# Up-projection by one level of Strassen's scheme in an encoder layer's MLP; its result goes through DRAM and the down-projection is a phase of its own

## Chip, cores and metric

The kernel runs on one core of a Trainium2 chip. The time is device microseconds of one execution, as the median of the runs shown: 2044.52 us (three runs, 2044.26 to 2045.95).

## What is computed

One layer of a hybrid encoder for 1024 prompt tokens and 8 x 16 sample tokens, 1152 rows in all, width 1024, inner MLP width 4096, in fp32. Attention, a gated delta network and their merge come first; the change touches only the channel mixer at the end, which runs on both groups of tokens:

```python
def channel_mixer(x, pre_g, post_g, w_up, w_down):
    h = rmsnorm(x, pre_g)
    u = jnp.square(jax.nn.relu(h @ w_up))
    return x + rmsnorm(u @ w_down, post_g)
```

## The kernel before

Every large product is made of three matmuls on TensorE. An fp32 operand is split into a high part in the type fp32r (`hi`, an ACT cast, L326) and the remainder (`lo`, a DVE subtraction, L327); `mm3` (L147-150) adds hi x hi, hi x lo and lo x hi in one PSUM accumulator. All matmuls named L150 are such.

Tokens are nine tiles of 128 (NTT), the width is eight pieces of 128 (KT), the inner width 32 rows of 128, each called an ft. The normalised input h stands transposed in SBUF as `hhi` and `hlo` [128, 9, 8, 128], in a pool on the right side of SBUF. The trace names these two `mhi` and `mlo` in this part of the program.

The out-projection stage (L1171-1216) goes tile by tile: 48 matmuls of 512 columns, a norm, the residual x1 stored to DRAM (L1209), a second norm (L158-175, its last operation L174), and eight 128x128 transposes (L183) whose results an ACT cast (`mhi`, L186) and a DVE subtraction (`mlo`, L187) write. A tile's transposes are emitted four tiles later than its matmuls (LAG).

The MLP (L1219-1288) is eight blocks of four ft. For each ft the up half loads two 256 KB pieces of w_up (L335, SP's queue), splits them, and runs 72 matmuls of 384 columns, 24 for each third of the tokens (`gemm_t`). Each third is evacuated by an ACT Relu (L1235) and a POOL square (L1236), and split into `uhi` and `ulo`, which stay in SBUF for the block. Two pieces of w_down (L1246) are split into `dhi` and `dlo`. The down half runs 18 accumulators (nine token tiles by two halves of the width), 12 matmuls of 512 columns each (L1260-1263); ACT copies the result to `yacc` in the first block (L1268) and DVE adds it in the others (L1270). Beside the last block the post-norm and the output go tile by tile.

Within an engine the order is set by a scheduler from the order of the code and from priorities (`high_priority`); buffers of a pool come free tile by tile (`reuse_waits="tile"`). All loads and stores of this part are issued by SP in one order, and an issue that waits holds back what stands behind it. Matmul accumulators rotate over PSUM banks, four with the tag `mm` in the up half; a bank is written again when its evacuation has read it.

## Time and profile before

| | |
|---|---|
| median of three runs | 2044.52 us |
| profiled execution | 2042.67 us |
| its span in the profile | 2041.0 us |
| PE busy | 1959.9 us, 96% |
| weight loads (PEld) busy, beside the matmuls | 1769.8 us |
| DVE / ACT / POOL busy | 1010.0 / 839.7 / 317.5 us |
| first down-projection matmul of the MLP | 1283.63 us |
| end of the last matmul | 2031.69 us |

The profile gives starts in microseconds from the start of the span. A matmul's listed duration is longer than the distance to the next start, since matmuls overlap in the array; what a stream of them costs is read from the starts. In a row of the grouped views the columns are: line, engine, operation, output<-inputs, shape, count, then busy time and mean ns, then the engine's idle time just before them with what ended it. In the views by window the columns are length, the busy time of PE, weight load, DVE, ACT and POOL with counts, the granted clock of TensorE, the share of the DMA engines' time, and GB/s.

### The profile page before, as it was taken

The page shows a single profiled execution, that of the slowest core. Times are in us where ns is not written, and L with a number is a line of the kernel's source. Part 1 is how long each engine was busy: PE and PEld are TensorE (multiplying, and loading weights), DVE is VectorE, ACT ScalarE, POOL GpSimd, SP SyncE. Part 2 cuts the span into 40 slices and gives each one's busy share as a digit, 9 for nine tenths or more (in the row PEclk, how much of TensorE's full clock was granted, in tenths as well). Part 3 has the DMA queues.
Part 4 walks back from the last instruction along what each step waited for, and adds up shares of the span by engine and source line. Part 5 has one row for each costly group of instructions (what it writes and reads, how often), then busy time and mean ns, then how long its engine had stood idle before and what let it go on. Part 6 is the DMA issues. An engine that isn't in the chain of part 4 may idle for free.

```text
span 2041.0 us, 29371 instructions
## 1 busy us (share of the span) xinstructions
PE 1959.9 (96%) x10892; PEld 1769.8 (87%) x10892; DVE 1010.0 (49%) x2403; ACT 839.7 (41%) x1982; POOL 317.5 (16%) x453
## 2 busy tenths in 40 slices
PE   7989999999999899999899999999999999999998
PEld 6979898898898878778789789898989898989896
DVE  6457577775765476666454465032323232323227
ACT  5433464654636475655443445240303030303032
POOL 1141332513312200000022001010101010202010
PEclk9999999999999999999999999999999999999999
DMA  6142324224253643433553522020202020202024
GB/s 191 44 102 62 101 62 118 67 76 129 53 141 104 188 148 103 130 100 83 168 156 96 173 106 93 1 83 1 83 1 83 1 83 11 73 11 73 21 83 155
DMA packets 216300, 181.47 MB, mean 89 GB/s; under 512 B 51132, under 2 KB 193272, under 8 KB 216156
## 3 DMA queue, kind: packets, MB, share of 16 engines
q1 hardware_dynamic: 201888, 160.33, 27.6%
q10 hardware_dynamic: 14268, 19.25, 2.6%
q8 instruction: 86, 1.41, 0.3%
q14 instruction: 58, 0.48, 0.1%
HBM read 136.67 MB, written 42.87 MB: 88 GB/s over the span
## 4 chain that ended last, share of the span: by engine, by line
PE 79%; DMA 7%; DVE 5%; ACT 4%; issue 3%; POOL 1%; SPq 1%; DVEq 0%; ACTq 0%; POOLq 0%
PE mm L150 48%; PE mf L150 13%; PE pc L1011 2%; PE pa L150 1%; DMA wor<-in_w_out_dram 1%; PE pd L150 1%; PE pb L150 1%; PE pc L150 1%; DVE xs L610 1%; PE pe L150 1%; DMA be<-rows_o 1%; PE mm L1040 1%; PE pc L625 1%; PE mm L1061 1%; PE pb L1002 1%
## 5 line engine op out<-in xcount | busy, mean ns | idle before, releaser
L150 PE MATMUL mf<-hhi,wlo 128*128 128x384 f32 x744 | 262.6, 353 | 3.4 <-DVE wlo L327 3.4
L150 PE MATMUL mf<-hhi,whi 128*128 128x384 f32 x744 | 261.6, 352 | 1.8 <-ACT gst L211 1.8
L150 PE MATMUL mf<-hlo,whi 128*128 128x384 f32 x744 | 262.5, 353 | 0.0
L150 PE MATMUL mm<-mlo,whi 128*128 128x384 f32 x768 | 260.1, 339 | 0.3 <-DVE mlo L187 0.3
L150 PE MATMUL mm<-mhi,whi 128*128 128x384 f32 x768 | 260.3, 339 | 0.0
L150 PE MATMUL mm<-mhi,wlo 128*128 128x384 f32 x768 | 260.1, 339 | 0.0
L150 PE MATMUL mm<-dhi,ulo 128*128 128x512 f32 x576 | 224.1, 389 | 0.0
L150 PE MATMUL mm<-dlo,uhi 128*128 128x512 f32 x576 | 224.1, 389 | 0.0
L150 PE MATMUL mm<-dhi,uhi 128*128 128x512 f32 x576 | 224.1, 389 | 0.0
L1236 POOL TENSOR_TENSOR ur<-ur 128x384 f32<-128x384 f32 x96 | 84.1, 877 | 776.2 <-ACT ur L1235 657.2
L1270 DVE TENSOR_TENSOR yacc<-mm,yacc 128x512 f32<-128x512 f32 x126 | 87.1, 691 | 203.7 <-PE mm L150 203.0
L327 DVE TENSOR_TENSOR wlo<-raw,whi 128x512 fp32r<-128x512 f32 x166 | 115.6, 697 | 110.3 <-ACT whi L326 106.6
L326 ACT CAST dhi<-raw 128x512 fp32r<-128x512 f32 x64 | 38.9, 620 | 293.3 <-PE mm L150 269.9
L327 DVE TENSOR_TENSOR ulo<-ur,uhi 128x384 fp32r<-128x384 f32 x96 | 53.7, 560 | 211.0 <-ACT uhi L326 211.0
L326 ACT CAST whi<-raw 128x512 fp32r<-128x512 f32 x166 | 102.8, 620 | 118.8 <-PE mm L150 47.0
L150 PEld LDWEIGHTS mf<-hhi,wlo 128*128 128x128 f32 x744 | 141.9, 191 | 4.6 <-DVE wlo L327 4.3
L150 PEld LDWEIGHTS mm<-mlo,whi 128*128 128x128 f32 x768 | 144.2, 188 | 0.8 <-DVE mlo L187 0.5
L150 PEld LDWEIGHTS mm<-mhi,whi 128*128 128x128 f32 x768 | 144.2, 188 | 0.6 <-ACT whi L326 0.3
L150 PEld LDWEIGHTS mm<-mhi,wlo 128*128 128x128 f32 x768 | 144.2, 188 | 0.3 <-DVE wlo L327 0.3
L150 PEld LDWEIGHTS mf<-hhi,whi 128*128 128x128 f32 x744 | 141.9, 191 | 2.4 <-ACT gst L211 2.1
L150 PEld LDWEIGHTS mf<-hlo,whi 128*128 128x128 f32 x744 | 142.1, 191 | 0.7
L150 PEld LDWEIGHTS mm<-dhi,ulo 128*128 128x128 f32 x576 | 108.1, 188 | 22.5
(470 smaller groups left out, 4049.9 us busy)
## 6 DMA issues: line engine op xcount, KB each, us to landing
raw<-in_w_in_dram SPq DMA_DIRECT2D x86, 256.0 KB
raw<-in_w_up_dram SPq DMA_DIRECT2D x64, 256.0 KB
raw<-in_w_down_dram SPq DMA_DIRECT2D x64, 256.0 KB
gate_d<-gst ACTq DMA_DIRECT2D x48, 192.0 KB
ga<-gate_d SPq DMA_DIRECT2D x48, 192.0 KB
xt<-in_x_prompt_dram SPq DMA_DIRECT2D x16, 512.0 KB
fr_d<-gst ACTq DMA_DIRECT2D x36, 192.0 KB
y<-rows_n SPq DMA_DIRECT2D x16, 288.0 KB
```

Of the source, the lines that this page charges most:

```text
L150: T.matmul(out, a, b, start=first and i == 0, stop=last and i == n - 1)
L326: A.copy(h, raw)
L327: V.tensor_tensor(l, raw, f(h), ALU.subtract)
L610: (A.copy if h else V.tensor_copy)(xs[0:64, h], st_[64 * h:64 * h + 64])
L625: T.matmul(po[:, i * P:(i + 1) * P], xs[k0:].rearrange("p h c -> p (h c)"), qa[k0:, u].rearrange("p h c -> p (h c)"), start=True, stop=True)
L1002: T.transpose(tp[:, jj * 256 + qi * P:jj * 256 + qi * P + P], pr[qi][:, j * P:(j + 1) * P], ident)
L1011: T.matmul(acc[:, q0:256], v2[:, 2 * jp + jj, P * hh:P * hh + P], q[:, jj * 256 + q0:jj * 256 + 256], start=jp == 0 and jj == 0 and k == 0 ...
L1040: T.matmul(a[32 * b:32 * b + 32, P:384], qbd[:, b].rearrange("p h t -> p (h t)"), kt, start=True, stop=True)
L1061: T.matmul(o[:, bs], vc[:, 2 * b + i], pT[:, 1 + i, bs], start=False, stop=b == 3 and i == 1)
L1236: G.tensor_tensor(r, r, r, ALU.mult)
L1270: V.tensor_tensor(yacc[:, t, ns], acc, yacc[:, t, ns], ALU.add)
```

## The change

The up-projection takes the ft two by two (after four ft that are done in the old way). The product of a pair is seen as a 2x2 block product: the inner dimension 1024 in two halves of 512, the outputs in two ft of 128, and the tokens in two halves, namely the first and the second 64 columns of each token tile. Winograd's form of Strassen's scheme makes the four output blocks from seven block products instead of eight. It needs four sums of weight blocks (POOL, `w_ops`, for each pair) and four sums of blocks of h (`h_sums`, once, split into THI and TLO, which the program calls `th`). The 576 columns of a block are done in two groups, five tiles (320 columns) and four tiles (256 columns), 12 matmuls each: 168 matmuls a pair where there were 144 of 384 columns. The products that use blocks of h itself read five or four pieces of 64 columns; those that use `th` read consecutive columns. The running sums are made when a product is evacuated: ACT copies for the first, 14 DVE additions, then ACT Relu and ACT Square into `u`, a row of 1152 columns, which is stored to DRAM (`u_d`). All eight PSUM banks serve as accumulators in this part.

The down-projection starts when all pairs are done. Its pool `fin` takes the place of `hhi`, `hlo` and `th`. It loads each row of `u` from DRAM again, splits it, loads and splits w_down, and runs the same matmuls as before: eight blocks, 18 accumulators of 12 matmuls, and the same post-norm.

```diff
     wps.close()
-    wps_["w"] = ctx.enter_context(tc.tile_pool(name="wp2", bufs=1, reuse_waits="tile"))
+    wps2 = ctx.enter_context(ExitStack())
+    wps_["w"] = wps2.enter_context(tc.tile_pool(name="wp2", bufs=1, reuse_waits="tile"))
...
+    u_d = dr.tile([DFF // P, P, NT], F32, name="u_d")
+    TH = NTT * 64
+    GR = ((0, 5), (5, 9))
+    def halves_t(x):
+        return x.rearrange("p (t n) -> p t n", n=64)
+    ts_ = ctx.enter_context(ExitStack())
+    th = ts_.enter_context(tc.tile_pool(name="th", bufs=1, side="right", reuse_waits="tile"))
+    THI, TLO = ([th.tile([P, 4, TH], F32R, name=nm("th")) for _ in range(4)] for _ in range(2))
+    wps2.close()
+    with tc.tile_pool(name="up", bufs=1, reuse_waits="tile") as up:
+        wps_["w"] = up
+        WBUFS["w"] = (6, 5)
+        def h_sums(t0, t1):
+            n = t1 - t0
+            def B(h, i, j):
+                return f(h[:, t0:t1, 4 * i:4 * i + 4, 64 * j:64 * j + 64])
+            def tmp():
+                z = up.tile([P, 4, P], F32, tag="ws", bufs=3, name=nm("ws"))
+                return z.rearrange("p k (t n) -> p (k t n)", t=2).rearrange("p (t k n) -> p t k n", t=2, k=4)[:, :n]
+            def diff(a, b):
+                x, y = tmp(), tmp()
+                G.tensor_tensor(x, B(hhi, *a), B(hhi, *b), ALU.subtract)
+                G.tensor_tensor(y, B(hlo, *a), B(hlo, *b), ALU.subtract)
+                V.tensor_tensor(x, x, y, ALU.add)
+                return x
+            def rest(a, x):
+                y = tmp()
+                V.tensor_tensor(y, B(hhi, *a), x, ALU.subtract)
+                V.tensor_tensor(y, y, B(hlo, *a), ALU.add)
+                return y
+            def out(i, x):
+                hi, lo = (z[i][:, :, 64 * t0:64 * t1].rearrange("p k (t n) -> p t k n", n=64) for z in (THI, TLO))
+                split(x, hi, lo)
+            t1_ = diff((0, 1), (0, 0))
+            out(0, t1_)
+            t2_ = rest((1, 1), t1_)
+            out(1, t2_)
+            out(2, diff((1, 1), (0, 1)))
+            out(3, rest((1, 0), t2_))
+        N0 = 4
+        for ft in range(N0):
+            u = up.tile([P, NT], F32, tag="u", bufs=3, name=nm("u"))
+            def evu(c, acc, u=u):
+                cs = slice(c * CH, (c + 1) * CH)
+                A.activation(u[:, cs], acc, AF.Relu)
+                A.activation(u[:, cs], u[:, cs], AF.Square)
+            gemm_t(weights(halves(w_up[0], ft * P)), hhi, hlo, KT, evu, tag=("mm", 4))
+            S.dma_start(u_d[ft], u)
+            if ft == 0:
+                for t in range(0, NTT, 2):
+                    h_sums(t, min(t + 2, NTT))
+        banks()
+        def w_ops(pr):
+            with tc.high_priority(200):
+                a = {}
+                for i in range(2):
+                    for j, src in enumerate(halves(w_up[0], (2 * pr + i) * P)):
+                        a[i, j] = up.tile([P, 4, P], F32, tag="wr", bufs=6, name=nm("wr"))
+                        S.dma_start(a[i, j], src.rearrange("(k p) n -> p k n", p=P))
+            def add(x, y, op):
+                z = up.tile([P, 4, P], F32, tag="ws", bufs=3, name=nm("ws"))
+                G.tensor_tensor(z, x, y, op)
+                return z
+            def parts(x):
+                h, l = (up.tile([P, 4, P], F32R, tag="w" + z, bufs=5, name=nm("w" + z)) for z in "hl")
+                split(x, h, l)
+                return h, l
+            with tc.high_priority(100):
+                yield parts(a[0, 0])
+                s1 = add(a[1, 0], a[1, 1], ALU.add)
+                s2 = add(s1, a[0, 0], ALU.subtract)
+                yield parts(s2)
+                yield parts(add(a[0, 0], a[1, 0], ALU.subtract))
+                yield parts(a[1, 1])
+                yield parts(s1)
+                yield parts(add(a[0, 1], s2, ALU.subtract))
+                yield parts(a[0, 1])
+        def hop(i, j):
+            return (lambda k, t0, t1: [z[:, t0:t1, 4 * i + k, 64 * j:64 * j + 64] for z in (hhi, hlo)])
+        def top(i):
+            return (lambda k, t0, t1: [z[i][:, k, 64 * t0:64 * t1] for z in (THI, TLO)])
+        prods = (hop(0, 0), top(1), top(2), top(3), top(0), hop(1, 1), hop(1, 0))
+        for pr in range(N0 // 2, DFF // P // 2):
+            uu = [up.tile([P, NT], F32, tag="u", bufs=3, name=nm("u")) for _ in range(2)]
+            sm = [[], []]
+            for i, ((wh, wl), b) in enumerate(zip(w_ops(pr), prods)):
+                for c, (t0, t1) in enumerate(GR):
+                    n = 64 * (t1 - t0)
+                    o = pt("mm", 8)[:, :n]
+                    mm3(o, [p3 for k in range(4) for hi, lo in (b(k, t0, t1),) for p3 in (
+                        (wh[:, k], hi), (wh[:, k], lo), (wl[:, k], hi))])
+                    def plus(x, tag, r=None):
+                        if r is None:
+                            r = up.tile([P, 320], F32, tag=tag, bufs=2 + (tag == "sr"), name=nm(tag))[:, :n]
+                        if x is None:
+                            A.copy(r, o)
+                        else:
+                            V.tensor_tensor(r, o, x, ALU.add)
+                        return r
+                    def done(row, half, r):
+                        A.activation(r, r, AF.Relu)
+                        u = uu[row].rearrange("p (t n) -> p t n", n=P)[:, t0:t1, 64 * half:64 * half + 64]
+                        A.activation(u, halves_t(r), AF.Square)
+                    z = sm[c]
+                    if i == 0:
+                        z.append(plus(None, "s1"))
+                    elif i == 1:
+                        z.append(plus(z[0], "s2"))
+                    elif i == 2:
+                        z.append(plus(z[1], "s3"))
+                    elif i == 3:
+                        done(1, 0, plus(z[2], "sr"))
+                    elif i == 4:
+                        plus(z[1], None, z[1])
+                        done(1, 1, plus(z[2], None, z[2]))
+                    elif i == 5:
+                        done(0, 1, plus(z[1], None, z[1]))
+                    else:
+                        done(0, 0, plus(z[0], "sr"))
+            for i in range(2):
+                S.dma_start(u_d[2 * pr + i], uu[i])
+    ts_.close()
+    phs.close()
+    banks()
     FB = 4
-    with tc.tile_pool(name="up", bufs=1, reuse_waits="tile") as up:
-        yacc = None
+    fin = ctx.enter_context(tc.tile_pool(name="fin", bufs=1, side="right", reuse_waits="tile"))
+    yacc = fin.tile([P, NTT, D], F32, name="yacc")
+    gpost = fin.tile([P, D], F32, name="gpost2")
+    lss = fin.tile([P, 4], F32, name="lss")
+    lsq = fin.tile([P, 512], BF16, name="lsq")
+    dn = fin
+    if True:
         nb = DFF // (FB * P)
-        fin = None
         for blk in range(nb):
             us, wd = [], []
             for i in range(FB):
                 ft = blk * FB + i
-                urs = [up.tile([P, CH], F32, tag="ur", bufs=3, name=nm("ur")) for _ in range(3)]
-                uhi = up.tile([P, NT], F32R, tag="uhi", bufs=FB, name=nm("uhi"))
-                ulo = up.tile([P, NT], F32R, tag="ulo", bufs=FB, name=nm("ulo"))
-                def evu(c, acc, uhi=uhi, ulo=ulo, urs=urs):
-                    cs = slice(c * CH, (c + 1) * CH)
-                    r = urs[c]
-                    A.activation(r, acc, AF.Relu)
-                    G.tensor_tensor(r, r, r, ALU.mult)
-                    split(r, uhi[:, cs], ulo[:, cs])
-                gemm_t(weights(halves(w_up[0], ft * P)), hhi, hlo, KT, evu, tag=("mm", 4))
-                us.append((uhi, ulo))
                 with tc.high_priority():
-                    dhi = up.tile([P, D], F32R, tag="dhi", bufs=FB, name=nm("dhi"))
-                    dlo = up.tile([P, D], F32R, tag="dlo", bufs=FB, name=nm("dlo"))
+                    uhi = dn.tile([P, NT], F32R, tag="uhi", bufs=2 * FB, name=nm("uhi"))
+                    ulo = dn.tile([P, NT], F32R, tag="ulo", bufs=2 * FB, name=nm("ulo"))
+                    ur = dn.tile([P, NT], F32, tag="ur", bufs=2, name=nm("ur"))
+                    S.dma_start(ur, u_d[ft])
+                    split(ur, uhi, ulo)
+                    us.append((uhi, ulo))
+                    dhi = dn.tile([P, D], F32R, tag="dhi", bufs=2 * FB - 1, name=nm("dhi"))
+                    dlo = dn.tile([P, D], F32R, tag="dlo", bufs=2 * FB - 1, name=nm("dlo"))
                     for n in range(2):
                         ns = slice(n * 512, (n + 1) * 512)
-                        raw = wps_["w"].tile([P, 512], F32, tag="wr", bufs=2, name=nm("raw"))
+                        raw = dn.tile([P, 512], F32, tag="wr", bufs=2, name=nm("raw"))
                         S.dma_start(raw, w_down[0][ft * P:(ft + 1) * P, ns])
                         split(raw, dhi[:, ns], dlo[:, ns])
                 wd.append((dhi, dlo))
-            if blk == nb - 1:
-                phs.close()
-                fin = ctx.enter_context(tc.tile_pool(name="fin", bufs=1, side="right", reuse_waits="tile"))
-                gpost = fin.tile([P, D], F32, name="gpost2")
+            last = blk == nb - 1
+            if last:
                 S.dma_start(gpost, g_mlp_post[0].partition_broadcast(P))
-                lss = fin.tile([P, 4], F32, name="lss")
-                lsq = fin.tile([P, 512], BF16, name="lsq")
-            if yacc is None:
-                yacc = up.tile([P, NTT, D], F32, name="yacc")
             for t in range(NTT):
                 ts_ = slice(t * P, (t + 1) * P)
                 for n in range(2):
@@ -1262,7 +1407,7 @@
                     acc = mmt()
                     mm3(acc, [pr for (uh, ul), (dh, dl) in zip(us, wd) for pr in (
                         (uh[:, ts_], dh[:, ns]), (uh[:, ts_], dl[:, ns]), (ul[:, ts_], dh[:, ns]))])
-                    end = fin and t == NTT - 1
+                    end = last and t == NTT - 1
                     with tc.high_priority(200 if end else 0):
                         if blk == 0:
                             A.copy(yacc[:, t, ns], acc)
@@ -1270,7 +1415,7 @@
                             V.tensor_tensor(yacc[:, t, ns], acc, yacc[:, t, ns], ALU.add)
                     if end:
                         A.activation(lsq, yacc[:, t, ns], AF.Square, accum_out=lss[:, n:n + 1])
-                if not fin:
+                if not last:
                     continue
```

The change moves instructions at three places. The first is the beginning of the MLP. These are TensorE's rows there in the old order; `tp` are the transposes of the last token tiles, `mm_13279` an accumulator of the first ft:

```order
L150 MATMUL mm_13279<-mlo,whi_13246 128x384
L150 MATMUL mm_13279<-mhi,wlo_13247 128x384
L183 MATMUL tp_13214<-ident,mix_13083 128x128 x4
L150 MATMUL mm_13279<-mhi,whi_13246 128x384
L183 MATMUL tp_13221<-ident,mix_13083 128x128 x4
L150 MATMUL mm_13279<-mlo,whi_13246 128x384
L150 MATMUL mm_13279<-mhi,wlo_13247 128x384
L150 MATMUL mm_13308<-mhi,whi_13240 128x384
```

And in the new order:

```order
L183 MATMUL tp_13200<-ident,mix_12994 128x128 x4
L183 MATMUL tp_13207<-ident,mix_12994 128x128 x4
L183 MATMUL tp_13214<-ident,mix_13083 128x128 x4
L183 MATMUL tp_13221<-ident,mix_13083 128x128 x4
L150 MATMUL mm_13259<-mhi,whi_13249 128x384
L150 MATMUL mm_13259<-mlo,whi_13249 128x384
L150 MATMUL mm_13286<-mhi,whi_13249 128x384
```

The up matmuls no longer stand between the transposes but behind the last of them. On ACT the cast of the first w_up piece (`whi_13249`) stands behind the last `mhi` cast and the first `th` cast of the sums:

```order
L186 CAST mhi<-tp_13207 128x512
L186 CAST mhi<-tp_13214 128x512
L186 CAST mhi<-tp_13221 128x512
L326 CAST th_13234<-ws_13341 128x2x4x64
L326 CAST whi_13249<-raw_13247 128x512
L326 CAST whi_13255<-raw_13253 128x512
```

On SP the load of that piece, which stood among the loads of the out-projection's weights, now stands behind the last store of x1.

The second place is the end of a pair on TensorE, shown with waits. `mm_14819` is the last group of 256 columns of one pair; its first matmul stands in its place, and its other eleven stand behind product 4 of the next pair (`mm_15015` is that product's second group). The last rows of this are:

```order
L150 MATMUL mm_14819<-mhi,wh_14798 128x256
L150 MATMUL mm_14819<-mlo,wh_14798 128x256
L150 MATMUL mm_14819<-mhi,wl_14799 128x256
L150 MATMUL mm_15038<-mhi,wh_15034 128x320 [waits DVE_49,Activation_49]
L150 MATMUL mm_15038<-mlo,wh_15034 128x320
L150 MATMUL mm_15038<-mhi,wl_15035 128x320
```

The group behind it, `mm_15038`, uses the bank of `mm_14819`. Its wait for DVE is the wait for the addition that reads `mm_14819`. Such a place is there for each pair but the last.

The third place is the border between the phases, on SP, with waits. `u_17287` and `u_17286` are the last pair's rows, `ur` the reloaded rows, `raw` pieces of w_down:

```order
L1367 DMA u_d<-u_17287 128x1152 [waits DMAHW4_49,Activation_49]
L1367 DMA u_d<-u_17286 128x1152 [waits DMAHW5_49,Activation_49]
L1389 DMA ur_17574<-u_d 128x1152 [waits DMAHW6_49,PE_49]
L1389 DMA ur_17590<-u_d 128x1152 [waits DMAHW7_49,PE_49]
L1397 DMA raw_17580<-in_w_down_dram 128x512 [waits DMAHW0_49,PE_49]
L1397 DMA raw_17584<-in_w_down_dram 128x512 [waits DMAHW1_49]
L1402 DMA gpost_17569<-in_norm_mlp_post_dram 128x1024 [waits DVE_49,DMAHW2_49,PE_49,Pool_49]
L1389 DMA ur_17606<-u_d 128x1152 [waits DMAHW6_49,DMAHW3_49,DVE_49]
L1389 DMA ur_17622<-u_d 128x1152 [waits DMAHW7_49,DMAHW4_49,DVE_49]
L1397 DMA raw_17596<-in_w_down_dram 128x512 [waits DMAHW5_49,DMAHW0_49,DVE_49]
```

All loads of the down phase stand behind the stores of the last pair, where the loads for a block stood beside its up half before. The third `ur` waits for DVE, which frees its buffer.

## Prediction

> **What bounds the kernel now.** I read the page first, then the chain of waits, then the MLP stage in windows, then single matmul starts.
>
> ```profile
> span 2041.0 us, 29371 instructions
> PE 1959.9 (96%) x10892; PEld 1769.8 (87%) x10892; DVE 1010.0 (49%) x2403; ACT 839.7 (41%) x1982; POOL 317.5 (16%) x453
> 1240.86 0.70 DVE mlo L187
> 1241.57 0.04 issue
> 1241.61 4.26 PE mm L150 x23
> 1245.87 0.01 issue
> 1245.88 785.81 PE mm L150 x3960
> 1300.00:1400.00 100.00, 100.00 (x506) 91.59 (x505) 21.13 (x33) 28.95 (x53) 10.49 (x12) 1.00 0.15 43
> ```
>
> The chain's last link is TensorE alone: 3960 matmuls from 1245.88 to 2031.69 without a gap. A window inside it (columns: length, then busy time of PE, weight load, DVE, ACT, POOL, then clock, DMA share, GB/s) has PE at 100 of 100, full clock, the other engines under a third, DMA at 43 GB/s. So the MLP is worth what its matmuls cost, and a removed matmul pays at once, as long as nothing else becomes late. Here are the starts of the first matmul of down block 0, up block 1 and down block 1:
>
> ```profile
> 1283.63 0.39 PE L150 MATMUL mm<-dhi,uhi 128*128 128x512 f32 x1
> 1332.64 0.34 PE L150 MATMUL mm<-mhi,whi 128*128 128x384 f32 x1
> 1383.52 0.39 PE L150 MATMUL mm<-dhi,uhi 128*128 128x512 f32 x1
> 908.39 0.28 PE L1011 MATMUL pc<-plo,v 128*128 128x256 f32 x1
> 908.51 0.28 PE L1011 MATMUL pc<-phi,v 128*128 128x256 f32 x1
> 908.63 0.28 PE L1011 MATMUL pc<-plo,v 128*128 128x256 f32 x1
> ```
>
> A down block is 49.01 us for 216 matmuls of 512 columns, 226.9 ns each. An up block is 50.88 us for 288 matmuls of 384, 176.7 ns each. The attention's 256-column matmuls start 120 ns apart.
>
> **1. The matmuls that go.** The line through 256 and 512 columns has (226.9-120)/256 = 0.418 ns a column. It gives 146.7 ns at 320, and 173.4 at 384. The up matmuls take 176.7, and read their tokens from hi/lo tiles in three pieces of 128; I put the 3.3 ns on the two extra pieces, 1.65 ns each. In the new scheme four of seven products read whole rows (the sums in `th`): 12 x (146.7+120) ns = 3.20 us each. Three read `mhi`/`mlo` in five and four pieces of 64: 12 x (146.7+4x1.65+120+3x1.65) = 3.34 us each. A pair of ft is then 22.8 us, against 144 x 176.7 = 25.44 us: 2.62 us saved, times 14 pairs = **-36.7 us**. The ends: no price for pieces, 7 x 3.20, -42.6; the price on all seven, -28.8.
>
> The Trainium skill ("TensorE: Matmul & The Clock Gate", Part 2, "Back-to-back issue gap") has the isolated spacing as N/2.4 GHz plus about 2.5 ns, thus 109 ns at 256 columns. By it, with 136 ns at 320, a pair would be 20.6 us and this term -68 in place of -36.7. The trace disagrees with it, 120 ns measured, and I stay with the rows.
>
> **2. The start of the MLP.** Now the first up matmuls stand between the last transposes:
>
> ```profile
> 1134.43 0.43 SPq L335 DMA_DIRECT2D raw<-in_w_up_dram  x1
> ...
> 1222.42 13.29 SPq L1209 DMA_DIRECT2D x_d<-xt  x2
> 1242.18 0.99 SPq L335 DMA_DIRECT2D raw<-in_w_up_dram  x2
> 1245.20 0.62 ACT L326 CAST whi<-raw 128x512 fp32r<-128x512 f32 x1 [0.22 <-DMA raw<-in_w_up_dram]
> 1238.16 1.28 DVE L174 SCALAR_TENSOR_TENSOR mix<-xt,nss,gpre 128x1024 f32<-128x1024 f32 x1
> 1240.24 0.59 ACT L186 CAST mhi<-tp 128x512 fp32r<-128x512 f32 x1 [2.28 <-PE tp L183]
> 1242.67 0.69 DVE L187 TENSOR_TENSOR mlo<-tp,mhi 128x512 fp32r<-128x512 f32 x1
> L326 ACT CAST dhi<-raw 128x512 fp32r<-128x512 f32 x56 | 34.0, 620 | 289.8 <-PE mm L150 269.9 <-DMA raw<-in_w_down_dram 19.5
> L327 DVE TENSOR_TENSOR dlo<-raw,dhi 128x512 fp32r<-128x512 f32 x56 | 38.2, 692 | 67.7 <-ACT dhi L326 67.4
> L326 ACT CAST uhi<-ur 128x384 fp32r<-128x384 f32 x85 | 43.6, 513 | 83.6 <-POOL ur L1236 83.6
> L327 DVE TENSOR_TENSOR ulo<-ur,uhi 128x384 fp32r<-128x384 f32 x85 | 47.5, 559 | 194.9 <-ACT uhi L326 194.9
> L1235 ACT ACTIVATE ur<-mm 128x384 f32<-128x384 f32 x85 | 41.7, 490 | 83.3 <-PE mm L150 83.3
> L1236 POOL TENSOR_TENSOR ur<-ur 128x384 f32<-128x384 f32 x85 | 74.3, 874 | 628.8 <-ACT ur L1235 628.8
> ```
>
> The first up weights are loaded at 1134, long ahead. In the change the up pool opens after the out-projection stage: its first load stands on SP behind the last x1 store, whose issue ends at 1235.7, and its cast on ACT behind the last `mhi` cast and a first `th` cast, which waits for a DVE add behind the last `mlo`. All transposes go first. The norm of the last tile ends at 1239.44 as now; without the two `dhi` casts that stand between its two `mhi` casts, the last `mlo` ends near 1242.2 rather than 1243.4. Then the add (0.7), the `th` cast (0.62) and the `whi` cast (0.62) with their semaphores: the first up matmul at **1244.2**. The load, some 3 us from issue to use (1242.18 to 1245.20), is there by 1239 and hidden. Four plain ft take 50.88 us as now and end at 1295.1 where today's end at 1283.63: +11.4. Four loads of 256 KB leave the stage around 1134, worth nothing to 1 us there, I take -0.7. PE is nearly idle for up to 10 us; what that does to its clock is seen at 1016:
>
> ```profile
> 1016.00:1020.00 4.00, 2.24 (x6) 1.94 (x7) 1.97 (x4) 1.81 (x4) 0.00 (x0) 0.50 0.75 229
> 1020.00:1024.00 4.00, 3.54 (x10) 2.73 (x10) 2.30 (x4) 1.83 (x5) 0.00 (x0) 0.50 0.67 212
> 1024.00:1028.00 4.00, 3.71 (x13) 2.31 (x12) 2.30 (x4) 2.10 (x4) 0.00 (x0) 0.75 0.67 215
> 1019.15 0.53 PE L150 MATMUL pd<-ohi,whi 128*128 128x384 f32 x1
> 1019.47 0.53 PE L150 MATMUL pd<-olo,whi 128*128 128x384 f32 x1
> ```
>
> The granted clock is 0.50 and the 384-column matmuls start 0.32 us apart, not 0.17; full clock returns only after some us of dense work. I take one such stretch, 3.4 us of work at half clock that would take 1.7, so +1.7 (nothing to 3.4). The start is **+12.4 us**, 9 to 16. `h_sums` itself lies on DVE, ACT and POOL beside the plain ft (about 7.5 us for each of its five groups, done before 1295); without that cover each group would cost its 7.5.
>
> **3. The end of each pair.** Program order on PE leaves eleven matmuls of a pair's last group until after product 4 of the next pair; the next group reuses that bank and waits until DVE has read it. From the last start: the drain beyond the pace 0.28-0.12 = 0.16, the 256-column add (559 less 128 x 1.04 ns a column from the two lo rows) 0.43, two semaphores: 0.7 us, for 13 pairs **+9.1 us**. Queued behind it are the rest of this pair's matmuls, so nothing covers it. Ends: 0, if PE's queue hides it, and 18, if the add also finds a 0.69 us lo split ahead of it on DVE. Beside this the pair's own work fits: DVE 7 x 0.69 + 7 x 0.49 + 7 x 0.43 = 11.3 us, ACT 7 x 0.62 + 18 x some 0.4 = 11.5, POOL four 128x512 (874 ns at 384, so about 1.1) = 4.4, each within 22.8. Loads and stores are 2.2 MB a pair, about 97 GB/s. The 96 POOL squares that go were beside full PE: nothing.
>
> **4. Between the phases.** All down-phase tiles lie where `mhi`, `mlo` and `th` lay, and SP has the last pair's two stores ahead of the first `u` load. So no load starts before the last product is evacuated: add 0.43, Relu 0.38, Square 0.38, semaphores: the last store issues 1.45 us after the product's end.
>
> ```profile
> 741.28 5.35 DMA qv<-fr_d
> 811.31 7.31 DMA qv<-fr_d
> qv<-fr_d SPq DMA_DIRECT2D x8, 576.0 KB
> 10.00:20.00 10.00, 5.45 (x23) 4.10 (x23) 8.21 (x26) 7.22 (x16) 6.46 (x22) 1.00 0.96 298
> ```
>
> `qv` is a 576 KB load, the size of a `u` row. The first takes 5.4 us behind one issue: landed at +6.9; the second row and two w_down pieces share the queue at up to 298 GB/s: the last at +10.1. Casts of 1152 columns are 620 + 640 x 0.84 = 1.16 us on ACT, 1.36 on DVE. First down matmul +10.4, first ft done +14.2. Only two `ur` and two raw buffers exist and four banks, so PE can do four of 18 accumulators ft by ft (2.7 us of work), at about 6.3 us for an ft (lo split, issue, 2.8 us load, cast; the bytes alone, 1.6 MB with the loads between, are 5.6). Fourth ft done +33.1; then 14 accumulators x 12 x 226.9 ns = 38.1: block 0 ends at +71.2, not +49.0: +22.2. Idle and sparse work halve the clock here also, some 3.5: **+25.8 us**. Ends: 17.7 without the clock and with loads at the window's rate; 34 with each load like the 7.31 row and two clock stretches.
>
> **5. Later borders.** Two `u` rows and the fourth w_down of the next block stand behind a block's last accumulator: some 0.3 us x 7 = **+2**, 0 to 6. The tail from 2031.69 to 2041.0 keeps its instructions: 0.
>
> **Sum.** -36.7+12.4+9.1+25.8+2 = +12.6. The span would be 2053.6. The profiled execution is 1.67 us longer than its span, 2042.67, and 1.85 below the runs' median of 2044.52; on the median it is 2057.1. **Forecast 2057 us.**
>
> **The rivals.**
>
> A. The new waits are hidden, and the kernel is faster. Place: the pairs' ends and the phase border. Price: 0 for 9.1 and 17.7 for 25.8, together 17.2 less: **2040 us**. It decides once 3 and 4 cost under 23 us together instead of 35. For it: 43 GB/s leaves the queue free, and PE does run ahead in its own queue. Against it: the order lets no load pass the last store, and a bank can't be written before it is read. Chance 0.13.
>
> B. The phase border is bound by DMA: loads of 7.31 us, block 0 waits for each ft, 34 us: **2065**. For it, the 7.31 row; against, the 256 KB loads of 3 us. Chance 0.18.
>
> C. Weight loads set the pace of narrow matmuls.
>
> ```profile
> L150 PEld LDWEIGHTS mm<-mhi,whi 128*128 128x128 f32 x673 | 126.3, 188 | 0.3
> ```
>
> A load is 188 ns, more than the 120 of a 256-column matmul. If loads couldn't overlap, 168 x 188 = 31.6 us a pair, 8.8 more: +123, **2180**. The three starts 0.12 us apart, each with another stationary, speak against it. Chance 0.03.
>
> D. The matmul costs its columns alone, 0.418 x 256 = 107 and 0.418 x 320 = 134 ns: a pair 20.2 us, 2.6 less: -36, **2021**. It decides from a 256-column spacing of 0.11 us; the rows show 0.12. Chance 0.04. The Trainium skill's spacing named in part 1 is of this kind.
>
> E. The change doesn't do what it says: the program still issues 144 matmuls of 384. Its order on PE has the groups of 320 and 256, 168 a pair. Without the saving: 2094. Chance 0.01.
>
> **How the numbers follow.** The forecast holds 0.61; its own range, from ends that don't all fall together, is 2047 to 2067. With A and B: **2039 to 2074**; outside are C, D, E and the far ends of the costs in 2 to 4, about 0.2. A measurement of this kernel can tell about 0.2%, 4 us, from no change. Faster: D 0.04 and over half of A, 0.12. Same, 2040.4 to 2048.6: the rest of A and the low end of the forecast, 0.13. Slower: 0.75.
>
> **What would show it.** Right: 320- and 256-column matmuls 147 to 153 and 120 to 125 ns apart; first up matmul near 1244; a PE gap of 0.7 us once a pair, released by the DVE add; a PE gap of some 10 us before the first `dhi` matmul, then bursts of 2.7 us every 6. Wrong: 256-column matmuls over 0.13 us apart (saving gone), no gap at the pairs, or a border gap under 6 us.

## The result, and the profile after

The changed kernel takes 2053.97 us (median of nine runs), the kernel before 2044.38 us (nine runs): a ratio of 1.0052, 95% interval 1.0032 to 1.0071. That is 9.6 us or 0.5% slower; 2057 was forecast.

The page of the changed kernel has a longer span and a less busy TensorE:

```profile
span 2052.0 us, 30792 instructions
PE 1933.3 (94%) x11228; PEld 1733.7 (84%) x11228; DVE 1146.8 (56%) x2627; ACT 920.9 (45%) x2160; POOL 335.3 (16%) x433
```

PE has 26.6 us less work, as the change wants it, in a span 11.0 us longer. Where the chain of waits had one link of 786 us, it now is cut into pieces (start, duration, what):

```profile
1361.77 22.35 PE mm L150 x167
...
1384.19 0.62 ACT wh L326
1384.83 22.26 PE mm L150 x167
...
1623.39 6.95 DMA ur<-u_d
...
1632.99 5.89 DMA ur<-u_d
...
1641.52 3.69 DMA ur<-u_d
...
1647.86 5.24 DMA ur<-u_d
...
1654.84 45.73 PE mm L150 x190
1700.58 342.13 PE mm L150 x1502
```

The timeline of PE, with what ended its idle time, has the borders of the stages: the last out-projection matmul, the first up matmul, the first wait in the plain ft, the first product, a wait at a pair's end, the last product, the first down matmul and the first one on the fourth ft:

```profile
1226.37 0.39 PE L150 MATMUL mm<-wo,mlo 128*128 128x512 f32 x1
1243.73 0.69 PE L150 MATMUL mm<-mhi,whi 128*128 128x384 f32 x1 [3.17 <-ACT whi L326]
1284.68 0.45 PE L150 MATMUL mm<-mhi,whi 128*128 128x384 f32 x1 [1.47 <-ACT u L1280]
1299.75 0.42 PE L150 MATMUL mm<-mhi,wh 128*128 128x320 f32 x1 [0.43 <-ACT u L1280]
1384.83 0.38 PE L150 MATMUL mm<-mhi,wh 128*128 128x320 f32 x1 [0.61 <-ACT wh L326]
1620.78 0.27 PE L150 MATMUL mm<-mhi,wl 128*128 128x256 f32 x1
1632.14 0.79 PE L150 MATMUL mm<-dhi,uhi 128*128 128x512 f32 x1 [11.09 <-ACT dhi L326]
1654.84 0.79 PE L150 MATMUL mm<-dhi,uhi 128*128 128x512 f32 x1 [4.21 <-ACT dhi L326]
```

From these starts the difference is put together. The program ahead of the MLP is nearly the same in all kernels here, but ends up to 10.5 us apart in their profiles (1226.37 here, 1227.57 before), so stages are counted from their own beginnings.

| term, us | forecast | measured | how |
|---|---|---|---|
| matmuls of 14 pairs | -36.7 | -45.0 | 1299.75 to 1620.90 is 321.15, less 13 waits; before 28 x 12.72 = 356.2 |
| waits at the pairs' ends | +9.1 | +9.9 | 13 distances of 0.88 less the pace of 0.12 |
| start, to the end of the four plain ft | +13.1 | +17.3 | 73.38 from the out-projection's last matmul; before 56.06 |
| out-projection and before | -0.7 | -1.2 | 1226.37 against 1227.57 |
| phase border and later borders | +27.8 | +29.9 | last product to last matmul's start, 421.4; before 1727 x 226.7 ns = 391.5 |
| sum | +12.6 | +10.9 | spans: 2052.0 - 2041.0 = 11.0 |

The -1.2 of the out-projection says nothing about the -0.7 that was forecast: it is far smaller than the distances between profiles there.

### The profile page after: what moved, and what is told of

The parts are those of the page before. It is cut to its first block, busy times and chain, and to the rows that moved or that the text cites. A ratio compares the mean times of both kernels' runs of the same rounds, so it can differ in the third digit from the quotient of the medians.

```text
span 2052.0 us, 30792 instructions
## 1 busy us (share of the span) xinstructions
PE 1933.3 (94%) x11228; PEld 1733.7 (84%) x11228; DVE 1146.8 (56%) x2627; ACT 920.9 (45%) x2160; POOL 335.3 (16%) x433
## 5 line engine op out<-in xcount | busy, mean ns | idle before, releaser
L150 PE MATMUL mm<-th,wh 128*128 128x256 f32 (+1 forms) x896 | 177.8, 294 | 0.0
L150 PEld LDWEIGHTS mm<-dhi,uhi 128*128 128x128 f32 x576 | 109.3, 191 | 44.9 <-ACT dhi L326 22.4
L150 PEld LDWEIGHTS mm<-th,wh 128*128 128x128 f32 x896 | 143.3, 188 | 0.0
L150 PE MATMUL mm<-th,wl 128*128 128x320 f32 x448 | 131.8, 294 | 0.0
L150 PEld LDWEIGHTS mm<-dlo,uhi 128*128 128x128 f32 x576 | 109.6, 190 | 25.9 <-DVE dlo L327 3.1
L326 ACT CAST uhi<-ur 128x1152 fp32r<-128x1152 f32 x32 | 36.4, 1156 | 178.6 <-PE mm L150 132.5
L150 PE MATMUL mm<-mhi,wh 128*128 128x320 f32 (+1 forms) x336 | 97.8, 297 | 8.4 <-ACT wh L326 7.3
L150 PE MATMUL mm<-hhi,whi 128*128 128x384 f32 x288 | 103.6, 360 | 2.1 <-ACT whi L326 2.1
L150 PE MATMUL mm<-hhi,wlo 128*128 128x384 f32 x288 | 101.1, 351 | 1.7 <-DVE wlo L327 1.7
L150 PE MATMUL mm<-hlo,whi 128*128 128x384 f32 x288 | 102.6, 356 | 0.0
```

Of the source, the lines that this page charges most:

```text
L150: T.matmul(out, a, b, start=first and i == 0, stop=last and i == n - 1)
L326: A.copy(h, raw)
```

## The experiments

The expectations quote spans; a span in a profile lies some 2 us under the run's time. Below, "from the out-projection" is the span less the start of the out-projection's last matmul, so that the jitter of what lies ahead drops out: 813.4 us before, 825.6 after.

### e1_order: the pair's last group in its place

The raised priority of the weight sums stood around the `yield`s of a generator. While the generator sleeps, the loop that uses it emits its matmuls, and so at the raised priority too; the next pair then begins at about the same numbers as this one, and the last group of a pair competes with the next pair's. The edit raises the priority only while the sums are emitted:

```diff
-            with tc.high_priority(100):
-                yield parts(a[0, 0])
-                s1 = add(a[1, 0], a[1, 1], ALU.add)
+            def sums(f):
+                with tc.high_priority(100):
+                    return f()
+            yield sums(lambda: parts(a[0, 0]))
+            s1 = sums(lambda: add(a[1, 0], a[1, 1], ALU.add))
...
```

> The weight sums of a pair are made under a raised priority only while they are emitted; the pair's matmuls keep the running priority, so the last group of 256 columns is no longer left until after product 4 of the next pair. Theory (the late group holds a weight buffer and a bank; the ACT cast into that buffer can start only when it ends): the 13 gaps of 0.88 us between starts go, 13 x 0.76 = 9.9 us, and the span is 2042, about 0.5% below the changed kernel. Rival (the pair is bound by its evacuation on DVE and ACT, and the gap only shows it): the wait comes back elsewhere in the pair, the pair stays at 22.9 to 23.0 us and the span within 3 us of 2052.

Measured: span 2038.4; 814.97 from the out-projection, 10.6 less than after. The pairs take 311.1 us instead of 321.2, and no distance between starts over 0.45 us is left in them. The median is 2040.76 us; the ratio to the kernel before is 0.9987 (0.9966 to 1.0009), no difference that can be told. The theory holds: without the late group there are no waits, and the evacuations fit beside the matmuls.

### e11_six_w and e12_seven_w: what the late group holds

The profile after shows something that the prediction did not have: in 12 of the 13 places the matmul behind the late group waits for the ACT cast `wh`, not for DVE. The theory: the late group still reads its weights, and the cast writes into that buffer.

```diff
-                h, l = (up.tile([P, 4, P], F32R, tag="w" + z, bufs=5, name=nm("w" + z)) for z in "hl")
+                h, l = (up.tile([P, 4, P], F32R, tag="w" + z, bufs=6, name=nm("w" + z)) for z in "hl")
```

In the second, 7 stands for 6; the room comes from two instead of three u rows, and in the second from four instead of six raw pieces.

> Six instead of five buffers for the split weights of the up phase (and two u rows instead of three, for the room); the late group stays where it was. The theory of the prediction (the group behind the late one waits for the DVE addition that frees its bank): the distance between starts at that place stays with DVE, 0.16 + 0.43 and two semaphores, 0.7 us or a little more. The theory from the trace of the changed kernel (it waits for the ACT cast into the weight buffer that the late group holds, 0.62 us plus two semaphores, and the addition is done earlier): with a sixth buffer the cast no longer waits, the distance falls from 0.88 us to the DVE one, about 0.7 us, 13 x 0.18 = 2.3 us in all. If it stays at 0.88 us with ACT as the releaser, neither is right.

> Seven buffers for the split weights (four raw pieces instead of six, two u rows). In e11_six_w the cast still waited for the late group. Theory: that group belongs to product 6, the waiting one to product 5 of the next pair, six products on, so with six buffers it still takes the late group's; the seventh takes ACT out of that place's waits, DVE's addition is left, and the distance between starts falls from 0.88 to 0.7 us with DVE as the releaser. Rival (the cast waits for TensorE for another reason): 0.88 us with ACT again. Either way the time falls by at most 2.5 us.

The same matmul in the two timelines, first with six buffers, then with seven:

```profile
1382.04 0.38 PE L150 MATMUL mm<-mhi,wh 128*128 128x320 f32 x1 [0.61 <-ACT wh L326]
1387.41 0.41 PE L150 MATMUL mm<-mhi,wh 128*128 128x320 f32 x1 [0.52 <-DVE sr L1343]
```

With six the distance stays at 0.89 us and ACT is the releaser: my count of the buffers was one short, a miss. With seven it is 0.80 us and DVE's addition is the releaser, as the prediction had it. Both waits were there, ACT's 0.1 us longer, and taking one away shows the other. The cast is not needed for the full distance, though: in the last of the 13 places of the changed kernel, and in all 13 of e2_start and of e8_dve (four weight buffers, see below), DVE's addition is the releaser and the distance is 0.88 to 0.89 us. Why it is less, 0.80, in e12_seven_w is open. Only the order takes both. Each of the two is one run; from the out-projection they take 824.9 and 826.2 us, and no gain can be told.

### e3_raw4, e5_xt and e10_rows: the border between the phases

```diff
-                        raw = dn.tile([P, 512], F32, tag="wr", bufs=2, name=nm("raw"))
+                        raw = dn.tile([P, 512], F32, tag="wr", bufs=4, name=nm("raw"))
```

> Four instead of two buffers for the raw w_down pieces of the down phase. SP's order then has block 0's four u rows and eight w_down pieces as its first twelve loads (4.5 MB), and the rows of block 1, gpost and xt behind them. Theory (the border is bound by bytes, 9.6 MB at about 300 GB/s before the fourth ft is complete, half of which block 0 doesn't need): the fourth ft's first matmul comes some 20 us after the last product instead of 34, and the span falls by 12 us to 2040. Rival (the border is a latency loop through two u buffers: load, cast, subtraction, next issue): the u buffers are still two, the span falls by 4 us or less.

Measured: span 2039.6, 810.97 from the out-projection, 14.6 less than after. The chain at the border has two links of w_down pieces instead of four of u rows:

```profile
1627.95 5.75 DMA raw<-in_w_down_dram
...
1634.61 5.96 DMA raw<-in_w_down_dram
...
1641.27 46.74 PE mm L150 x204
1688.02 342.29 PE mm L150 x1502
```

The fourth ft begins 21.6 us after the last product instead of 33.95. The ratio to the kernel before is 0.9982 (0.9965 to 0.9999). But the edit does two things: it gives the pieces buffers, and it puts block 1's rows behind block 0's pieces. So the two other runs take bytes away and leave the two buffers. In e5_xt the residual `xt` takes the rotating `ur` buffers, so that its loads can't come early:

```diff
-                xt = fin.tile([P, D], F32, tag="xt", bufs=4, name=nm("xt"))
+                xt = dn.tile([P, NT], F32, tag="ur", bufs=2, name=nm("xt"))[:, :D]
```

> Only the place of the residual's buffers is changed: xt takes the two rotating u buffers, so that its loads can't be issued in block 0. The w_down pieces keep two buffers and block 1's u rows keep their place. Bytes theory of the border: three xt loads of 0.52 MB fewer before the fourth ft is complete, 1.6 MB at 300 GB/s, so its first matmul comes 29 us after the last product instead of 34, and the span falls by 5 us. Loop theory (what run e3_raw4 removed was the wait of a w_down piece for one of two buffers, not bytes): the fourth ft stays at 33 to 34 us, and the span within 1.5 us.

e10_rows adds to this four instead of eight buffers for `uhi` and `ulo`, which keeps two u rows of block 1 out of block 0:

```diff
-                    uhi = dn.tile([P, NT], F32R, tag="uhi", bufs=2 * FB, name=nm("uhi"))
-                    ulo = dn.tile([P, NT], F32R, tag="ulo", bufs=2 * FB, name=nm("ulo"))
+                    uhi = dn.tile([P, NT], F32R, tag="uhi", bufs=4, name=nm("uhi"))
+                    ulo = dn.tile([P, NT], F32R, tag="ulo", bufs=4, name=nm("ulo"))
```

> Four instead of eight buffers for the split u rows, and xt in the rotating u buffers; the w_down pieces keep two buffers. Before the fourth ft is complete, two u rows of block 1 and the xt loads are gone, 2.7 MB of 9.6. Theory from e5_xt (the border is the loop of w_down pieces through two buffers: issue, load, cast, subtraction): the fourth ft's first matmul stays at 30 us or more after the last product. Bytes theory (block 1's rows ahead of block 0's pieces): 6.1 MB to 6.9 MB at 300 GB/s, 23 to 26 us. Later blocks, whose rows now wait for a free buffer, may be slower; that isn't read here.

| | MB moved before the fourth ft | GB/s | fourth ft, us after the last product |
|---|---|---|---|
| after | 9.66 | 284 | 33.95 |
| e5_xt | 8.32 | 258 | 32.20 |
| e10_rows | 6.83 | 229 | 29.64 |
| e3_raw4 | 6.10 | 281 | 21.61 |

(Bytes are those of all DMA packets that begin between the last product and the fourth ft's first matmul. e5_xt and e10_rows are one run each.) At 284 GB/s, 8.32 MB would be 29.3 us and 6.83 MB 24.0; with two buffers the time falls by less, and the queue moves fewer bytes a second. So neither theory of mine holds alone. In e10_rows the long wait at the border is ACT's, for a piece of w_down:

```profile
1647.14 1.26 ACT L326 CAST dhi<-raw 128x512 fp32r<-128x512 f32 x2 [5.84 <-DMA raw<-in_w_down_dram]
```

This is the window from just after the last store to the fourth ft in the changed kernel:

```profile
1623.00:1655.00 32.00, 13.96 (x37) 9.21 (x37) 13.82 (x14) 13.26 (x16) 0.00 (x0) 0.70 0.91 301
```

The changed kernel stands at both limits together: the queue is full (the window's last two columns: a DMA share of 0.91 and 301 GB/s), and just under it, as e10_rows suggests with its 29.64 us, lies the loop of w_down pieces through two buffers. Bytes alone bring 4.3 us of the 12.3, four buffers with the better order bring all; what the order alone would bring was not run. e10_rows is 2057.8 in span: at the later borders, where the rows come late, the distance between starts is up to 2.2 us.

### e2_start and e8_dve: the beginning of the MLP

e2_start keeps the small weight pool of the out-projection stage open for the first ft, and makes room for it in the up pool (two u rows, four raw pieces, four weight buffers, two `sr`):

```diff
-    wps2.close()
     with tc.tile_pool(name="up", bufs=1, reuse_waits="tile") as up:
-        wps_["w"] = up
-        WBUFS["w"] = (6, 5)
...
             gemm_t(weights(halves(w_up[0], ft * P)), hhi, hlo, KT, evu, tag=("mm", 4))
+            wps_["w"] = up
+            WBUFS["w"] = (4, 4)
```

> The small weight pool of the out-projection stage stays open and serves the first ft; the up pool is made smaller for it (two u rows, four raw pieces, four weight buffers, two sr). Up matmuls then stand between the transposes again. Theory A (the start costs its 16 us because the first up weights come late): the first Strassen product starts near 1288 instead of 1299.75, since only the 3.6 us of waits on evacuations behind the casts of the sums stay; span 2040. Theory B (the sums of h are themselves the chain, 53 us of DVE and POOL work in a row from 1242 to 1295): the plain ft end earlier, but the second product waits for its sum, and the span falls by 5 us or less, 2047 or more.

Measured: the first up matmul stands 1.0 us behind the out-projection's last instead of 17.4, and the plain ft end at 1281.9. But then PE waits:

```profile
1295.18 0.64 PE L150 MATMUL mm<-mhi,wh 128*128 128x320 f32 x1 [13.11 <-ACT u L1277]
1292.06 0.41 ACT L326 CAST th<-ws 128x256 fp32r<-128x256 f32 x1 [2.13 <-DVE ws L1257]
1294.65 0.47 ACT L1277 ACTIVATE u<-mm 128x384 f32<-128x384 f32 x1
```

The first product comes 69.37 us after the out-projection instead of 73.38, and the span falls by 2.8 us to 2049.2: theory B, but for the place. It is the first product that waits, not the second: the Relu that releases it stands on ACT behind the last cast of the sums (`th`), which waits for DVE, and behind a cast of a weight sum. So the 16 us were not the late weights alone; behind them lay the sums of h. The kernel after shows why these take so long. DVE's and POOL's timelines in one group of the sums:

```profile
1273.67 1.58 POOL L1252 TENSOR_TENSOR ws<-mhi 128x512 f32<-128x512 f32 x1 [2.53 <-DVE ws L1259]
1275.21 1.75 POOL L1253 TENSOR_TENSOR ws<-mlo 128x512 f32<-128x512 f32 x1
1274.02 1.78 DVE L1260 TENSOR_TENSOR ws<-ws,mlo 128x512 f32<-128x512 f32 x1
1276.99 0.69 DVE L1254 TENSOR_TENSOR ws<-ws,ws 128x512 f32<-128x512 f32 x1 [1.19 <-POOL ws L1253]
```

The DVE operation that falls beside POOL's takes 1.78 us, its like without one 0.69. e8_dve is e2_start with the four subtractions of a group on DVE:

```diff
-                G.tensor_tensor(x, B(hhi, *a), B(hhi, *b), ALU.subtract)
-                G.tensor_tensor(y, B(hlo, *a), B(hlo, *b), ALU.subtract)
+                V.tensor_tensor(x, B(hhi, *a), B(hhi, *b), ALU.subtract)
+                V.tensor_tensor(y, B(hlo, *a), B(hlo, *b), ALU.subtract)
```

> e2_start with the four subtractions of a group of the sums of h on DVE instead of POOL. Theory (a DVE operation takes 1.2 to 1.8 us instead of 0.68 where it lies beside a POOL operation, so POOL's help is worth little): all DVE operations of the sums take 0.68 us, the chain becomes 14 x 0.68 = 9.6 us a group instead of 11.8, and the gap before the first product shrinks from 13.45 us to 5 or less. Rival (POOL's share is real work taken off DVE): the chain gets longer, the gap is 13 us or more.

The same line (the last operation of a sum) in the grouped view from 1238 to 1296, first of e2_start, then of e8_dve:

```profile
L1257 DVE TENSOR_TENSOR ws<-ws,mlo 128x512 f32<-128x512 f32 x8 | 11.4, 1422 | 0.0
L1257 DVE TENSOR_TENSOR ws<-ws,mlo 128x512 f32<-128x512 f32 x8 | 5.5, 684 | 0.0
```

DVE has four operations more in each group, and is done sooner: the first product comes 56.25 us after the out-projection, 0.2 more than the end of the plain ft before, and in the second product one distance between starts is 2.06 us. From the out-projection it is 810.4 us, 12.9 less than e2_start. One profile and one run stand behind this, and e9_all repeats it.

### e4_plain: the phase separation alone

```diff
-        N0 = 4
+        N0 = 32
...
-            if ft == 0:
-                for t in range(0, NTT, 2):
-                    h_sums(t, min(t + 2, NTT))
```

> All 32 ft are done in the plain way and the sums of h are left out, so the down-projection as a phase of its own, with u through DRAM, is all that is left of the change. Theory (the phase separation and the late start cost 40 us and the pairs win 35): start and border stay, 12 and 30 us, and the 28 ft cost 12.5 us each instead of 11.5: span 2075 to 2082. Rival (the separation is cheap and the Strassen part is what loses): span 2045 or less.

```profile
1237.30 401.82 PE mm L150 x2304
```

Measured: 2075.54 us, a ratio of 1.0157 (1.0118 to 1.0197); span 2068.3, and 846.6 from the out-projection, 33.2 more than before. The span lies under the expected 2075 to 2082: the out-projection ended 4.6 us earlier in this profile than in the one after, and start and border came to 9.7 and 28.2 us instead of 12 and 30. The plain ft cost 12.55 us each instead of 12.72 before, which hides 4.8 us in 28 of them (see the last section). So the separation and the start cost 38 us, of which 33 show, and the pairs win back 21 in the changed kernel.

### e6_pairs_border, e7_six and e9_all: the edits together

e6_pairs_border has the edits of e1_order and e3_raw4. e7_six has these, that of e2_start and six plain ft (`N0 = 6`). e9_all has those of e1_order, e3_raw4, e2_start and e8_dve, with four plain ft.

> The edits of e1_order and e3_raw4 together. Theory (two separate waits on TensorE's own time): their gains add, 10 and 15 us, span 2027, 0.7% faster than the kernel before. Rival (the faster pairs store u later than the border needs it, or loads collide): one of the gains is lost, span 2036 or more.

> The edits of e1_order, e3_raw4 and e2_start together, and six plain ft instead of four, thirteen pairs. Theory (the sums of h are a chain of 53 us from 1240 to 1294, and 25 us more of plain matmuls cover the 13.45 us in which TensorE waited for it in e2_start): no gap of over 2 us at the first product; one pair less costs 2.7 us, the start's 14 go, and the span is 2027-14+3 = 2016, 1.2% faster than the kernel before. Rival (the first product waits for something else, such as its weights): a gap of 8 us or more stays there and the span is 2023 or more.

> The edits of e1_order, e3_raw4, e2_start and e8_dve together: pairs without the late group, four w_down buffers, the first up weights ahead, the sums of h on DVE alone; four plain ft. Theory (four separate waits on TensorE's time): against the end of the out-projection the gains were 10.7, 14.6 and 15.2 us (the last for e2_start with e8_dve); they add to 40.5, and the span is about 2052 - 40 = 2012, 1.5% faster than the kernel before and 8 us below e7_six. Rival (the sums on DVE delay the evacuations or the weight splits of the first pairs once these are closer together): 2020 or more, no better than e7_six.

| | span | from the out-projection | time, us | ratio to before (95%) |
|---|---|---|---|---|
| e6_pairs_border | 2024.2 | 800.8 | 2029.32 | 0.9949 (0.9925 to 0.9973) |
| e7_six | 2019.6 | 792.5 | 2021.11 | 0.9896 (0.9868 to 0.9925) |
| e9_all | 2017.9 | 785.7 | 2017.33 | 0.9879 (0.9856 to 0.9903) |

In e6_pairs_border the gains add: 825.6 - 800.8 = 24.8 of 10.6 + 14.6. In e7_six a wait of 4.7 us between starts stays inside the plain ft, released by a Relu that stands behind the sums' casts on ACT; its span is 3.6 above the expected one. In e9_all the gains add to 39.9 of the 40.4 that the parts had measured; the expected span of 2012 was missed because the out-projection ended 5.9 us later in this profile than in the one after. It is 1.2% faster than the kernel before. In e6_pairs_border all pairs are one link of the chain:

```profile
1296.93 311.27 PE mm L150 x2352
```

## Why the prediction was right

The sign and the size were right, and TensorE waited at the places that the order had shown. Inside each of the four steps something failed that the sum hides, since its errors went both ways: the pairs saved 8 us more, and start, pairs' ends and border cost 7 us more. That the sum came out within 2 us is luck to that extent.

**The matmuls.** A saving was forecast, -36.7 us, and it is -45.0. The chain's link of 2352 matmuls in 311.27 us is 22.23 us a pair, not 22.8. The step that failed is the price of the pieces: matmuls that read five or four pieces of 64 columns start 147 and 117 ns apart, and so do those that read whole rows. That is 5.9 us of the 8.3, the distance to the forecast's own end without a price, -42.6; the rest is the pace of the narrow matmuls, 117 to 118 ns where 120 was taken. Rival D, columns alone, would have given 20.2 us a pair and is out.

**The pair's end.** The step gave 0.7 us a pair; it is 0.76. The size stands, the releaser was half right: in 12 of 13 places the cast into the weight buffer comes last, with DVE's addition done 0.1 us before it, and in the runs with four or seven weight buffers it is the addition. I had looked at the bank and not at who else uses the late group's tiles.

**The start.** The first up matmul at 1244.2 was forecast, and 1243.73 measured; counted from the out-projection it came 17.4 us behind instead of 16.6. The half clock was there also: to 1247.0 the granted clock is 0.50, and matmuls start 0.32 us apart. What failed is "about 7.5 us for each of its five groups", and that the sums of h lie beside the plain ft at no cost. Their casts stand on ACT ahead of the Relus that free the four banks, and DVE and POOL wait for each other: 53 us for the five groups instead of 37.5, to 1295.4, so that the forecast's "done before 1295" nearly fits in spite of the wrong price. This shows as three waits up to 1299.75, 3.6 us together, and in e2_start as 13.45 us. The Trainium skill ("SBUF — State Buffer", section "Who interferes with whom") has a rule that I had not drawn on: a DVE instruction with two inputs in SBUF contends with a GpSimd instruction that reads SBUF, over a shared port pair that is an exclusive lock. The trace agrees: 0.68 us becomes 1.78 beside POOL, and the mean of one line falls from 1.42 to 0.684 in e8_dve.

**The border.** First down matmul +10.4 forecast, +11.25 measured. The four accumulators were to be through with the fourth ft at +33.1; they begin it at +33.95, and the next accumulator starts at +39.2, after twelve matmuls 0.43 us apart at a granted clock of 0.50. The rate was right, 284 GB/s near the 298 used; the bytes were not. The step counted 1.6 MB an ft, and 9.66 MB moved before the fourth, so that an ft took 7.6 us instead of 6.3. The sum of 27.8 with the later borders became 29.9: the later ones cost 1.6 us (the chain's last link, 1502 matmuls, is 342.1 us long, at 226.7 ns it would be 340.5), where 2 was forecast, and block 0 the other 28.3, where 25.8 was.

**The rivals.** A, hidden waits, did not happen by itself; but its condition, waits under 23 us, is what e6_pairs_border makes by hand, and the kernel is then faster. B, a border bound by DMA, is half true, as the runs on the border show. C is out at 117 ns a matmul, each with a weight load of its own; the attention's three starts were weaker evidence than the prediction says, since in the code two neighbours share their weights. E is out: the changed kernel issues 168 matmuls a pair, 2352 in all.

## What to carry to other kernels

A scheme that saves multiplications here saved 45 of 356 us and gave all of it back, and 11 us more, in three new waits, none of which the arithmetic shows: price the first and the last instruction of each new phase before the middle. When a phase is cut off, count the loads that its first block needs, in the order in which the queue will issue them, and see to it that the next block's don't stand between. Where a group is scheduled late, ask for every tile that it holds, not only for the one that the next wait names.

## What had not been expected of the hardware

The same matmul of 384 columns, in three pieces, has two paces. In the windows' count of matmuls, first two stretches of the kernel before, then one of the changed kernel and one of e1_order, whose plain ft are the same program:

```profile
1250.00:1280.00 30.00, 30.00 (x175) 30.00 (x175) 12.00 (x19) 13.39 (x26) 6.47 (x7) 1.00 0.35 106
1340.00:1370.00 30.00, 30.00 (x172) 30.00 (x171) 11.43 (x18) 12.74 (x24) 6.24 (x7) 1.00 0.30 88
1248.00:1276.00 28.00, 28.00 (x164) 28.00 (x163) 27.80 (x30) 11.25 (x22) 15.54 (x10) 1.00 0.26 78
1248.00:1276.00 28.00, 28.00 (x161) 28.00 (x160) 26.81 (x29) 11.21 (x21) 15.83 (x11) 1.00 0.22 69
```

By the starts it is 173.3 ns in the first and third row, and 176.7 in the others, at full clock and without a wait. Before, block 0 ran at the first pace and all later blocks at the second. It is 2%, or 6.9 us over the 2016 up matmuls of blocks 1 to 7 before, and may be part of what the pairs seem to save. No run was made to find what selects it. It also undoes the row on which the prediction put its price for pieces: at 173.3 ns three pieces lie on the line of 173.4 that the prediction drew without a price.
